# Residual tokens, P7's weights and the g_post products of the first output pair put into other places of a two-layer trunk's last stages

## The chip, the cores and the metric

The kernel runs on one core of a Trainium2 chip. The metric is the device time of one execution in microseconds (us), the lower the better; several executions are timed and the median is given. One further execution was recorded by the hardware profiler.

The engines that matter here are TensorE (PE: matmuls, and PEld: its weight loads), VectorE (DVE), ScalarE (ACT), GpSimd (POOL) and SyncE (SP, whose queue SPq issues most transfers between DRAM and the on-chip memory). Each engine executes its own instructions in the order in which they stand in its queue; an instruction that waits for a semaphore holds up all behind it on that engine.

## The reference

A trunk of two layers over 512 tokens of width 2048, all in float32. Each layer normalises its input, applies one combined input projection, runs a gated linear attention group and a chunked attention group, gates and concatenates their outputs, and applies one output projection, a second normalisation and the residual. The part that the change touches is the end:

```python
def hybrid_layer(x, w_in, w_out, g_pre, g_post, w_alpha, b_alpha, g_gla, g_att, rel_bias):
    B, S, _ = x.shape
    h = rmsnorm(x, g_pre)
    z = h @ w_in
    ...
    y = jnp.concatenate([o_gla, o_att], axis=-1) @ w_out
    return x + rmsnorm(y, g_post)

def rmsnorm(x, g):
    xf = x.astype(jnp.float32)
    y = xf * lax.rsqrt(jnp.mean(xf * xf, axis=-1, keepdims=True) + EPS) * g.astype(jnp.float32)
    return y.astype(x.dtype)
```

So the row sums of squares are taken over y before `g_post`, and the product with `g_post` may come before or after the scaling by the root.

## The kernel before

**Matmuls and jobs.** Every weight block is 2048 rows by 512 columns, cut into 8 chunks of 128 x 1024 (two rows of 128 x 512 side by side), 512 KB each. A float32 product is made of three: the weight chunk is split into `wh` (rounded, on ScalarE, line 195) and `wl` (the rest, on VectorE, line 203), the operand likewise, and TensorE adds hi by hi, hi by lo and lo by hi (line 384). A pair of blocks is computed with seven products P1 to P7 in place of eight; each product is four *jobs*, one for each chunk c = 0 to 3, and each job is 12 matmuls of 128 x 512. "P5 2" below is the job of P5 with chunk 2. P1 uses a weight chunk H alone; P5 and P6 add a second chunk `raw` into it (line 189); P3 uses P6's `raw`; P7 subtracts a chunk of its own from H (line 191); P2 and P4 use chunks of the first block. P5, P6, P3 and P7 also read sums of operands (`sa`, 512 KB, from the DRAM arrays oS), one tile for each job (line 176).

`Job.load` issues the transfers of a job on SyncE's queue, `Job.high` makes the addition or subtraction and `wh`, `Job.low` makes `wl`; they run a few jobs ahead of the matmuls. The buffers are rings: 4 for H, 5 for raw, 4 for sa, 4 for wh, 3 for wl, 8 for the small tiles t2 (128 x 512). A job's `wl` can be written when the matmuls of the job three before have read theirs.

**Output projection.** It has four blocks of 512 columns, in two pairs: W01 (columns 0 to 1023) and W23 (1024 to 2047). In both layers W01 goes through the seven products (`fast_gemm`); in the last layer W23 does too, in layer 0 it goes through `std_gemm`, one job after the other. The jobs of W23 in the last layer stand in this order:

```python
PROD_END = order("10 20 11 21 12 22 13 23 50 51 60 52 61 53 62 63 30 31 32 33 70 71 72 73 40 41 42 43")
```

The results come out as P2, P4, P3 and P7 finish, two token tiles each: `out_consume` calls `project`, which combines two results on VectorE (`combine`, line 341), takes the sum of squares on ScalarE (line 1301) and multiplies by `g_post` on VectorE (line 1304) into the slots `ys`: a122, a123, g8, g11 for W01 and g0 to g3 for W23. `finish_token` then forms the root, scales, adds the residual and writes the output. W01's gains are loaded into two tiles called bias in the linear-attention part of the layer; W23's are loaded into two t2 tiles at its start (line 1291).

**Residual tokens.** For token tiles 2 and 3 the layer's input is loaded into g9 and g10 (512 KB each) and into bias, bias, sg, sg (256 KB each): `load_tokens` lists the moves and `Tokens.load` issues some of them (line 452). In the last layer that is done behind P3 3 and P7's jobs (`residual`).

**P7's weights in W23.** They go to four spare slots, g12, g13, g16 and g17, and are fetched when P3's jobs are loaded.

**Order.** The order of the instructions on each engine is fixed when the program is built: a scheduler simulates a timeline and lines the instructions up in it; `tc.issue_after(x)` adds the condition that an instruction stands behind x. `pump` and `Pace` let side work (`tasks`, which yield) advance by steps between matmuls. `last_load`, `last_low`, `last_cast` and `last_mm` hold the latest instruction of that kind.

Of the kernel before, what the change touches and what calls it, by code (L numbers as in the profile page):

```python
# [7 lines left out]
F32 = mybir.dt.float32  # L8
# [7 lines left out]
P = 128  # L16
# [17 lines left out]
def hybrid_trunk(  # L34
# [30 lines left out]
    def nm(s):  # L65
        serial[0] += 1
        return f"{s}_{serial[0]}"
# [68 lines left out]
    last_cast, last_low, last_mm, last_load = [None], [None], [None], [None]  # L136

    class Job:
        def __init__(self, l, kind, c, b0, b1=None, pair=None):
# [13 lines left out]
        def load(self):  # L153
            k, c, p, b0, b1 = self.kind, self.c, self.pair, self.b0, self.b1
            end = b0 >= NB_IN and k != "std"
            if end:
                c = OC[c]
            top, bottom = (c + 4, c) if end else (c, c + 4)
            if k == "std":
                self.raw = self.fetch(rtile("raw", bufs=5), b0, c)  # L160
            elif k == "P1":
                p["H", self.c] = self.fetch(rtile("H"), b0, top)
            elif k == "P5":
                p["r", self.c] = self.fetch(rtile("raw", bufs=5), b1, top)
            elif k == "P6":
                p["r", self.c] = self.fetch(rtile("raw", bufs=5), b1, bottom)
            elif k == "P7":
                p["r", self.c] = p.pop(("t", self.c)) if b0 == W23[0] else self.fetch(rtile("raw", bufs=5), b0, top)
            elif k == "P2" or (k == "P4" and end):
                p["r", self.c] = self.fetch(rtile("raw", bufs=5), b0, bottom)  # L170
            sums = so_d if end else sa_d[self.l]
            src = sums.get((LEFT.get(k), c))
            if src is not None and b0 != NB_IN and not (k == "P5" and b0 == AV0):
                until(lambda: k == "P4" or (id(sums), LEFT[k], c) in written)
                self.a = rtile("sa", (2, 512), F32R)
                last_load[0] = nc.sync.dma_start(flat(self.a), src).ins
            if k == "P3" and b0 == W23[0]:
                with tc.issue_after(last_load[0]):
                    p["t", self.c] = self.fetch(slot(SPARE[self.c], [2, 512]), b0, c + 4)

        def high(self):
# [264 lines left out]
    XS1 = ("g9", "g10")  # L446

    class Tokens(list):
        def load(self, n=None):
            for z, src in self.moves[:n]:  # L450
                with tc.issue_after(last_load[0]):
                    nc.sync.dma_start(z, src)
            del self.moves[:n]

# [249 lines left out]
    def layer(l):  # L704
# [476 lines left out]
        def turn_gla(h, p):  # L1181
            ps = aux()
            for f in range(2):
                for tt in range(2):
                    nc.tensor.transpose(
                        ps[:, f * 256 + tt * P : f * 256 + (tt + 1) * P],
                        normed[h, p][:, tt, f * P : (f + 1) * P], ident,
                    )
            assert p or h >= 2 or ("P2", h) in passed
            op = slot(OG[p, h], [2, 512], F32R)  # L1190
            full_o = out_parts(h)[2 * p + 1]
            for f in range(2):
# [12 lines left out]

        def gla_heads(j, gvh, gvl):
            units = []
# [83 lines left out]
            nc.sync.dma_start(gp, bass.AP(tensor=src.tensor, offset=src.offset, ap=[[0, P], [1, W]]))  # L1291
            return gp

        def project(o, n, src, gp, between=None):
            if o not in ssy:
                ssy[o] = sm(5, "ssy", 4)
                nc.gpsimd.memset(ssy[o][:, 4:5], EPS)
            if (o, n // 2) not in ys:
                ys[o, n // 2] = slot(YS[n // 2][o], [1024])
            j = t2(dtype=BF16)  # L1300
            nc.scalar.activation(j, src, AF.Square, scale=D ** -0.5, accum_out=ssy[o][:, n : n + 1])
            if between is not None:
                between()
            nc.vector.tensor_tensor(
                out=ys[o, n // 2][:, (n % 2) * W : (n % 2 + 1) * W], in0=src, in1=gp, op=ALU.mult
            )

        def out_evac(n):
            gp = load_gain(n, t2())
# [42 lines left out]
        def out_consume(n):  # L1352
            if n:
                gains[:] = [load_gain(n + j, t2()) for j in range(2)]
            ends = []

            def f(j, h, t, src, comb):
                until(lambda: len(gains) == 2)
                o = 2 * h + t
                ending = last and n == 2 and (j, h) == (0, 1)  # L1360

                def begin():
                    ends.append(finish_token(o, xs[1][t]))
                    next(ends[-1])

                with nullcontext() if n and (j, h) == (0, 1) else tc.issue_after(last_low[0]):
                    project(o, n + j, src if comb is None else comb(t2()), gains[j], begin if ending else None)
                if last and n == 2 and (j, h, t) == (1, 0, 1):
                    tasks.append(finish(0, None))
                if ending:  # L1370
                    if t == 0:
                        next(ends[0])
                    else:
                        for end in ends:
                            for _ in end:
                                pass
            return f

        fast_gemm(l, W01, out_consume(0), rate=2, after=lambda k, c: used.add((k, c)), end=True, ops=O)
        drain()  # L1380

        def residual(k, c):
            if (k, c) == ("P3", 3):
                xs[1] = load_tokens(1, x_src)
            elif k == "P7":
                xs[1].load(2 if c > 1 else 1)

        if last:
            fast_gemm(
# [3 lines left out]
        else:  # L1393
            for half in range(2):
                for b in W23:
                    if b == W23[1]:
                        xs[half] = load_tokens(half, x_src)
                        xs[half].load()
# [65 lines left out]
```

## Time and profile before

| | us |
|---|---|
| three runs | 1640.9, 1643.17, 1645.68 (median 1643.17) |
| profiled execution | 1639.9 |
| its span from first to last instruction | 1637.8 |
| TensorE busy | 1613.9 |
| VectorE busy | 1253.2 |
| ScalarE busy | 911.4 |
| GpSimd busy | 122.0 |

The mean granted clock of TensorE in the profiled execution is 0.997 of full speed. Rows of the timeline read: start (us from the span's start), busy us, engine, line and operation, output <- inputs with partitions x elements, count; in square brackets the idle time of the engine just before, and what released it. Rows of windows read: the stretch, its length, the busy time of PE, PEld, DVE, ACT and POOL with the number of instructions, then TensorE's granted clock, the share of the DMA engines that was busy, and what they moved in GB/s.

### The profile page before, as it was taken

The numbers are of one execution on the slowest core, as the hardware profiler recorded it, in microseconds if no ns is written. First come the engines' busy times: TensorE is split into PE (matmuls) and PEld (weight loads), VectorE is DVE, ScalarE is ACT, GpSimd is POOL, SyncE is SP. The second block draws the span as 40 slices with busy tenths as digits, with TensorE's granted clock in tenths as the row PEclk, the third lists the DMA queues.
The fourth block names the chain that finished last, engine by engine and source line by source line (L and its number), as shares of the span: only waits on it lengthen the run. The fifth ranks groups of instructions, "written<-read, shape, count | busy, mean of one in ns | idle before, by whom it ended". The sixth has DMA issues, their size and how long they took to land.

```text
span 1637.8 us, 24501 instructions
## 1 busy us (share of the span) xinstructions
PE 1613.9 (99%) x8986; PEld 1382.4 (84%) x8986; DVE 1253.2 (77%) x1630; ACT 911.4 (56%) x1497; POOL 122.0 (7%) x182
## 2 busy tenths in 40 slices
PE   9999999999999999999999999999999999999996
PEld 7888999998888778788788889999988887787885
DVE  5987778687787868995786667776776878699976
ACT  7554445666554556654674444455665545566553
POOL 0120000100000100000122000000000101101001
PEclk9999999999999999999999999999999999999999
DMA  9698685785869667277989486858858596785967
GB/s 368 239 377 283 229 308 196 251 305 173 297 201 354 223 220 262 95 262 267 332 278 398 172 309 220 305 184 271 272 175 296 186 333 232 232 297 200 347 232 228
DMA packets 130759, 426.10 MB, mean 260 GB/s; under 512 B 14052, under 2 KB 26852, under 8 KB 130608
## 3 DMA queue, kind: packets, MB, share of 16 engines
q1 hardware_dynamic: 115632, 370.22, 65.2%
q0 software_dynamic: 14432, 53.24, 8.8%
q8 instruction: 71, 1.16, 0.3%
q10 hardware_dynamic: 576, 1.08, 0.2%
q14 instruction: 48, 0.39, 0.1%
HBM read 371.25 MB, written 55.33 MB: 260 GB/s over the span
## 4 chain that ended last, share of the span: by engine, by line
PE 89%; DVE 5%; DMA 4%; issue 1%; ACT 1%; DVEq 0%; POOL 0%; SPq 0%; ACTq 0%; POOLq 0%
PE mm L384 46%; PE mm L374 19%; PE mm L306 12%; PE ax L907 2%; DVE wl L203 1%; PE ax L384 1%; PE ax L1092 1%; DMA H<-in_w_dram 1%; PE ax L890 1%; DMA raw<-in_w_dram 1%; DMA x_mid<-g 1%; PE ax L1064 1%; DVE g L106 1%; PE ax L871 1%; PE ax L870 1%
## 5 line engine op out<-in xcount | busy, mean ns | idle before, releaser
L384 PE MATMUL mm<-wh,sa 128*128 128x512 f32 x1472 | 479.1, 395 | 6.4 <-DMA sa<-oS 4.8
L195 ACT CAST wh<-raw 128x1024 fp32r<-128x1024 f32 (+1 forms) x249 | 261.3, 1053 | 223.1 <-PE mm L384 88.1
L203 DVE TENSOR_TENSOR wl<-raw,wh 128x1024 fp32r<-128x1024 f32 (+1 forms) x249 | 302.5, 1218 | 92.2 <-PE mm L384 31.6
L195 ACT CAST wh<-H 128x1024 fp32r<-128x1024 f32 x240 | 251.6, 1051 | 212.2 <-PE mm L384 96.8
L203 DVE TENSOR_TENSOR wl<-H,wh 128x1024 fp32r<-128x1024 f32 x240 | 292.9, 1222 | 91.8 <-PE mm L384 34.4
L384 PEld LDWEIGHTS mm<-wh,sa 128*128 128x128 f32 x1472 | 276.5, 188 | 74.1 <-issue 11.7
L384 PE MATMUL mm<-wl,sa 128*128 128x512 f32 x736 | 288.9, 392 | 4.3 <-DVE wl L203 4.3
L374 PE MATMUL mm<-sa,wh 128*128 128x256 f32 x1280 | 236.8, 285 | 0.0
L384 PE MATMUL mm<-wh,a 128*128 128x512 f32 x608 | 200.5, 394 | 0.5 <-ACT wh L195 0.5
L374 PEld LDWEIGHTS mm<-sa,wh 128*128 128x128 f32 x1280 | 200.0, 191 | 0.3
L374 PE MATMUL mm<-sa,wl 128*128 128x256 f32 x640 | 181.1, 283 | 0.0
L189 DVE TENSOR_TENSOR H<-H,raw 128x1024 f32<-128x1024 f32 x132 | 160.3, 1221 | 7.9 <-DMA raw<-in_w_dram 6.6
L384 PEld LDWEIGHTS mm<-wl,sa 128*128 128x128 f32 x736 | 138.7, 188 | 32.5 <-DVE wl L203 5.4
L384 PEld LDWEIGHTS mm<-wh,a 128*128 128x128 f32 x608 | 113.5, 188 | 24.4 <-ACT wh L195 0.9
L374 PEld LDWEIGHTS mm<-sa,wl 128*128 128x128 f32 x640 | 122.5, 191 | 0.0
L425 POOL TENSOR_TENSOR sm<-sm,mhalf 128x2 f32<-128x2 f32 (+2 forms) x42 | 52.8, 1258 | 934.3 <-DVE sm L917 452.5
L384 PE MATMUL mm<-wl,a 128*128 128x512 f32 x304 | 119.8, 394 | 0.0
L191 DVE TENSOR_TENSOR raw<-H,raw 128x1024 f32<-128x1024 f32 x56 | 68.6, 1225 | 45.2 <-DMA raw<-in_w_dram 45.0
L374 PE MATMUL mm<-a,wh 128*128 128x256 f32 x512 | 95.3, 285 | 0.0
L306 PE MATMUL mm<-wh,a 128*128 128x512 f32 x288 | 91.5, 390 | 0.0
L384 PE MATMUL mm<-wh,g 128*128 128x512 f32 x288 | 90.9, 390 | 0.2 <-ACT wh L195 0.2
L208 DVE TENSOR_TENSOR H<-H,raw 128x1024 f32<-128x1024 f32 x48 | 58.7, 1224 | 33.2 <-DMA raw<-in_w_dram 33.2
(235 smaller groups left out, 2429.3 us busy)
## 6 DMA issues: line engine op xcount, KB each, us to landing
raw<-in_w_dram SPq DMA_DIRECT2D x319, 512.0 KB, 4.9
sa<-S SPq DMA_DIRECT2D x184, 512.0 KB, 4.4
H<-in_w_dram SPq DMA_DIRECT2D x60, 512.0 KB, 5.1
sa<-A SPq DMA_DIRECT2D x48, 512.0 KB, 6.1
S<-g POOLq DMA_DIRECT2D x32, 512.0 KB, 8.9
sa<-oS SPq DMA_DIRECT2D x16, 512.0 KB, 5.9
oa<-g POOLq DMA_DIRECT2D x12, 512.0 KB, 6.4
g<-in_x_dram SPq DMA_DIRECT2D x10, 512.0 KB, 9.1
```

The source lines that it names most:

```text
L106: return nc.vector.tensor_tensor(out=lo, in0=src, in1=hi.bitcast(F32), op=ALU.subtract).ins
L189: nc.vector.tensor_tensor(out=h, in0=h, in1=r, op=ALU.add)
L191: nc.vector.tensor_tensor(out=r, in0=h, in1=r, op=ALU.subtract)
L195: last_cast[0] = nc.scalar.copy(self.wh[:, z, :], src[:, z, :]).ins
L203: last_low[0] = nc.vector.tensor_tensor(out=self.wl[:, z, :], in0=self.src[:, z, :], in1=self.wh[:, z, :].bitcast(F32), op=ALU.subtract).ins
L208: nc.vector.tensor_tensor(out=h, in0=h, in1=self.src, op=ALU.add)
L306: nc.tensor.matmul(pss[o], a(part, kk, o) if callable(a) else a[:, part, t], rhs[:, kk, :], start=(i == 0 and kk == 0 and m == 0), stop=(i ...
L374: nc.tensor.matmul(dst, lhs[:, kk, f], a[:, part, tok], start=(fresh and kk == 0 and m == 0 and ft % 2 == 0), stop=(c == 3 and kk == 1 and ...
L384: last_mm[0] = nc.tensor.matmul(out_ps[t], a[:, part, tok], rhs[:, kk, :], start=(fresh and kk == 0 and m == 0), stop=(c == 3 and kk == 1 ...
L425: nc.gpsimd.tensor_tensor(out=out_r, in0=v, in1=mhalf[:, : v.shape[-1]], op=ALU.pow)
L870: nc.tensor.matmul(ps[:, :n], self.qh[:, t], self.kl[:, :n], start=False, stop=False)
L907: nc.tensor.matmul(o, self.pt[i][:, j * P : (j + 1) * P], av[hd // 4, j // 2][:, j % 2, (hd % 4) * P : (hd % 4 + 1) * P], start=(j == 0), ...
```

## The change

It has four parts.

1. In the last layer's W23, P7's own weights are fetched when P5's jobs are loaded, each behind `last_h`, the last H load of a P1 job, in place of when P3's jobs are loaded.
2. In the last layer the residual tokens are listed after P2 0, and one move is issued at each step of P1 and P2, behind `last_h`; before, they were listed after P3 3 and issued at P7's jobs. `Tokens.load` takes the instruction to stand behind as an argument.
3. W01 keeps y without `g_post`: the combination writes straight into the `ys` slot, P4's result is copied there by ScalarE, and the sum of squares reads y. W01's gains are no longer loaded in the linear-attention part, which leaves the bias tiles free for the tokens.
4. A task `late_gains`, put up in both layers when W01 is through, loads two gains into t2 tiles and multiplies the eight halves of W01's `ys` slots in place, one product after each three steps of the task, each behind `last_low`.

```diff
@@ -160,6 +160,7 @@
             elif k == "P1":
                 p["H", self.c] = self.fetch(rtile("H"), b0, top)
+                last_h[0] = last_load[0]
...
-            if k == "P3" and b0 == W23[0]:
-                with tc.issue_after(last_load[0]):
+            if k == "P5" and b0 == W23[0]:
+                with tc.issue_after(last_h[0]):
                     p["t", self.c] = self.fetch(slot(SPARE[self.c], [2, 512]), b0, c + 4)
@@ -446,9 +447,9 @@
     class Tokens(list):
-        def load(self, n=None):
+        def load(self, behind, n=None):
             for z, src in self.moves[:n]:
-                with tc.issue_after(last_load[0]):
+                with tc.issue_after(behind):
                     nc.sync.dma_start(z, src)
@@ -1198,10 +1199,6 @@
-            if len(og) == 8:
-                for n in range(2):
-                    gains.append(tmp.tile([P, W], F32, tag="bias", name=nm("bias"), bufs=2))
-                    load_gain(n, gains[n])
@@ -1291,19 +1288,32 @@
-        def project(o, n, src, gp, between=None):
+        def project(o, n, src, gp=None, comb=None, between=None):
...
+            dst = ys[o, n // 2][:, (n % 2) * W : (n % 2 + 1) * W]
+            y = src if comb is None else comb(dst if gp is None else t2())
+            if gp is None and comb is None:
+                nc.scalar.copy(dst, src)
             j = t2(dtype=BF16)
-            nc.scalar.activation(j, src, AF.Square, scale=D ** -0.5, accum_out=ssy[o][:, n : n + 1])
+            nc.scalar.activation(j, y, AF.Square, scale=D ** -0.5, accum_out=ssy[o][:, n : n + 1])
             if between is not None:
                 between()
-            nc.vector.tensor_tensor(
-                out=ys[o, n // 2][:, (n % 2) * W : (n % 2 + 1) * W], in0=src, in1=gp, op=ALU.mult
-            )
+            if gp is not None:
+                nc.vector.tensor_tensor(out=dst, in0=y, in1=gp, op=ALU.mult)
+
+        def late_gains():
+            gs = [load_gain(n, t2()) for n in range(2)]
+            for o in range(NT):
+                for n in range(2):
+                    for _ in range(3):
+                        yield
+                    dst = ys[o, 0][:, n * W : (n + 1) * W]
+                    with tc.issue_after(last_low[0]):
+                        nc.vector.tensor_tensor(out=dst, in0=dst, in1=gs[n], op=ALU.mult)
...
-                    project(o, n + j, src if comb is None else comb(t2()), gains[j], begin if ending else None)
+                    project(o, n + j, src, gains[j] if n else None, comb, begin if ending else None)
@@ -1378,12 +1387,13 @@
         fast_gemm(l, W01, out_consume(0), rate=2, after=lambda k, c: used.add((k, c)), end=True, ops=O)
         drain()
+        tasks.append(late_gains())
 
         def residual(k, c):
-            if (k, c) == ("P3", 3):
+            if (k, c) == ("P2", 0):
                 xs[1] = load_tokens(1, x_src)
-            elif k == "P7":
-                xs[1].load(2 if c > 1 else 1)
+            if k in ("P1", "P2") and xs:
+                xs[1].load(last_h[0], 1)
```

What this does to the order of SyncE's queue around the start of the last layer's W23, and of VectorE's some jobs later, is shown in three pieces. Names carry a tile's tag and a running number. First SyncE before the change, from the last H of W23's P1 jobs on:

```order
L150 DMA H_2956_15159<-in_w_dram 128x1024
L1291 DMA t2_2943_15115<-in_g_post_dram 128x512
L1291 DMA t2_2944_15117<-in_g_post_dram 128x512
L150 DMA raw_2966_15216<-in_w_dram 128x1024
L150 DMA raw_2970_15237<-in_w_dram 128x1024
L150 DMA raw_2974_15258<-in_w_dram 128x1024
L150 DMA raw_2980_15283<-in_w_dram 128x1024
L150 DMA raw_2990_15316<-in_w_dram 128x1024
```

The same place with the change:

```order
L150 DMA H_2944_15143<-in_w_dram 128x1024
L453 DMA g9_2945_15145<-x_mid_79 128x1024
L453 DMA g10_2946_15146<-x_mid_79 128x1024
L150 DMA g12_2958_15193<-in_w_dram 128x1024
L453 DMA bias_2947_15147<-x_mid_79 128x512
L150 DMA g13_2963_15218<-in_w_dram 128x1024
L453 DMA bias_2948_15148<-x_mid_79 128x512
L453 DMA sg_2949_15149<-x_mid_79 128x512
L150 DMA g16_2972_15266<-in_w_dram 128x1024
L1288 DMA t2_2929_15095<-in_g_post_dram 128x512
L1288 DMA t2_2930_15097<-in_g_post_dram 128x512
L1288 DMA t2_2938_15121<-in_g_post_dram 128x512
```

A fourth gain follows, and then the raws of P5 and P6; three of P7's four weights and five of the six token moves now stand between the last H and these raws. Before, both stood between the `sa` loads at the end of W23:

```order
L176 DMA sa_3010_15419<-oS40_134 128x1024
L150 DMA g16_3011_15421<-in_w_dram 128x1024
L150 DMA raw_3052_15604<-in_w_dram 128x1024
L452 DMA g10_3040_15556<-x_mid_79 128x1024
L150 DMA raw_3055_15626<-in_w_dram 128x1024
L176 DMA sa_3016_15443<-oS41_135 128x1024
L150 DMA g17_3017_15445<-in_w_dram 128x1024
L452 DMA bias_3041_15557<-x_mid_79 128x512
L452 DMA bias_3042_15558<-x_mid_79 128x512
L452 DMA sg_3043_15559<-x_mid_79 128x512
L176 DMA sa_3020_15463<-oS32_132 128x1024
```

These token moves and weights are gone from there with the change; only raws remain among the `sa` loads. On VectorE the eight late products (line 1316) stand, with the change, between the `wl` splits (line 204) of P2 3 and P6 1. From P2 3's split on, where `wl_2964` is P5 0's, `wl_2968` P5 1's and `wl_2975` P6 0's:

```order
L204 TENSOR_TENSOR wl_2959_15209<-raw_2953_15169,wh_2955_15187 128x1024
L1316 TENSOR_TENSOR a122_2859_14739<-a122_2859_14739,t2_2938_15121 128x512
L1316 TENSOR_TENSOR a123_2862_14745<-a123_2862_14745,t2_2938_15121 128x512
L1316 TENSOR_TENSOR a122_2859_14739<-a122_2859_14739,t2_2939_15123 128x512
L1316 TENSOR_TENSOR a123_2862_14745<-a123_2862_14745,t2_2939_15123 128x512
L204 TENSOR_TENSOR wl_2964_15234<-H_2906_14999,wh_2960_15212 128x1024
L1316 TENSOR_TENSOR g8_2910_15007<-g8_2910_15007,t2_2938_15121 128x512
L190 TENSOR_TENSOR H_2920_15051<-H_2920_15051,raw_2961_15214 128x1024
L190 TENSOR_TENSOR H_2906_14999<-H_2906_14999,raw_2966_15239 128x1024
L204 TENSOR_TENSOR wl_2968_15257<-H_2920_15051,wh_2965_15237 128x1024
L1316 TENSOR_TENSOR g8_2910_15007<-g8_2910_15007,t2_2939_15123 128x512
L192 TENSOR_TENSOR g12_2958_15193<-H_2906_14999,g12_2958_15193 128x1024
```

In this piece six late products and the first of P7's four subtractions (line 192, into g12) stand among the splits of P5; before, the products stood in W01 and this subtraction behind the `wl` of P3 0. The other subtractions stand, with the change, between the splits of P5 2 and P6 3; before, the last of them stood among those of P7.

More of the change, by code (lines that the diff above doesn't have):

```diff
@@ L135, in hybrid_trunk @@
     SPARE = ("g12", "g13", "g16", "g17")
-    last_cast, last_low, last_mm, last_load = [None], [None], [None], [None]
+    last_cast, last_low, last_mm, last_load, last_h = [None], [None], [None], [None], [None]
     class Job:
@@ L1357, in f @@
             def f(j, h, t, src, comb):
-                until(lambda: len(gains) == 2)
                 o = 2 * h + t
@@ L1397, in layer @@
                         xs[half] = load_tokens(half, x_src)
-                        xs[half].load()
+                        xs[half].load(last_load[0])
                     std_gemm(l, b, (2 * half, 2 * half + 1), OL, operand_out, out_evac(b - NB_IN), rate=3, lag=2)
```

## The prediction

> **What bounds the kernel now.** I read the page's head and engine totals first, then the waits of TensorE, then the timeline around the longest of them.
>
> ```profile
> span 1637.8 us, 24501 instructions
> PE 1613.9 (99%) x8986; PEld 1382.4 (84%) x8986; DVE 1253.2 (77%) x1630; ACT 911.4 (56%) x1497; POOL 122.0 (7%) x182
> ```
>
> TensorE is busy for 99% of the span, so only its holes can be won or lost (the profiled run took 1639.9 us, 2.1 outside the span). The waits of TensorE, as total, times and longest:
>
> ```profile
> PE mm L384 <- DMA sa<-oS: 4.8, 2, 3.2
> PE mm L384 <- DVE wl L203: 4.3, 2, 2.7
> ```
>
> The first is the only one on a transfer, and both its cases lie in the last layer's second output pair, W23:
>
> ```profile
> 1598.07 0.39 PE L384 MATMUL mm<-wh,sa 128*128 128x512 f32 x1
> 1601.66 0.47 PE L384 MATMUL mm<-wh,sa 128*128 128x512 f32 x1 [3.20 <-DMA sa<-oS]
> 1604.27 0.39 PE L384 MATMUL mm<-wh,sa 128*128 128x512 f32 x1
> 1606.25 0.47 PE L384 MATMUL mm<-wh,sa 128*128 128x512 f32 x1 [1.59 <-DMA sa<-oS]
> ```
>
> ```profile
> 1546.62 0.61 PE L384 MATMUL mm<-wh,a 128*128 128x512 f32 x2
> ...
> 1568.83 0.39 PE L384 MATMUL mm<-wl,sa 128*128 128x512 f32 x1
> ```
>
> The last two rows give TensorE's beat. From W23's first matmul to P5 0's first with wl lie 98 matmuls in 22.21 us: 0.227 each, 2.72 for a job of 12. Start to start the two gaps are 3.59 and 1.98; less one matmul each, they lose 3.36 + 1.75 = 5.1 us. Nothing behind them could take that up, as TensorE sets the end.
>
> Three stretches of W23 (length, then busy us of PE, PEld, DVE, ACT, POOL, clock, DMA share, GB/s) and SyncE's queue in the last tell why the sums were late:
>
> ```profile
> 1528.00:1550.00 22.00, 22.00 (x98) 18.20 (x97) 19.25 (x22) 13.06 (x23) 0.00 (x0) 1.00 1.01 396
> 1550.00:1582.00 32.00, 32.00 (x143) 26.48 (x142) 25.97 (x25) 14.97 (x18) 0.00 (x0) 1.00 0.59 190
> 1582.00:1608.00 26.00, 21.21 (x93) 16.98 (x92) 19.98 (x18) 11.28 (x14) 0.00 (x0) 1.00 0.97 362
> ...
> 1592.02 0.33 SPq L150 DMA_DIRECT2D g<-in_w_dram  x1
> 1593.82 1.64 SPq L452 DMA_DIRECT2D bias<-x_mid  x2
> ...
> 1597.75 0.32 SPq L176 DMA_DIRECT2D sa<-oS  x1
> ```
>
> ```profile
> DMA to landing us min/median/max: 3.6/7.8/10.5
> ```
>
> The DMA engines are full (0.97) from 1582 on and 0.59 busy before. The late sum is issued at 1597.75, and the sums of this stretch land a median 7.8 us after issue against 3.6 at best. Counted in SyncE's queue, 10.0 MB are issued there (8 sums, 4 of P7's weights and 3 raws of 0.52 MB, tokens of 2.1 MB), and 362 GB/s carry 9.4 in 26 us: the stretch is too short for them.
>
> **The change, part by part.**
>
> (a) P7's weights and the tokens move to the stretch around 1550. That takes 4 x 0.52 + 2.1 = 4.2 MB out of the full stretch; what stays, 5.8 MB, needs 16 of its 26 us. After the move each sum is behind raws alone in SyncE's queue. The latest of those raws wait until VectorE has read P6's raw tiles in P3, by my count at about 1595, and the sum behind needs to be there at 1602; even 4 us of landing fits. I take the whole 5.1 us as won. Its lower bound is one of the two waits, 3.36.
>
> (b) The transfers arrive where they are put. Ahead of the raws of W23's P5 and P6 now stand an H, most of the tokens, three of the four weights and four gains. Before, SyncE issued there:
>
> ```profile
> 1537.01 3.69 SPq L150 DMA_DIRECT2D H<-in_w_dram  x3
> 1540.81 1.61 SPq L1291 DMA_DIRECT2D t<-in_g_post_dram  x2
> ```
>
> ```profile
> DMA to landing us min/median/max: 9.0/9.0/9.0
> ```
>
> From the last H to the last gain that is 6 x 0.52 + 7 x 0.26 = 5.0 MB (H, two tokens, three weights; three small tokens, four gains). At the 396 GB/s of the full stretch, from about 1542 on with some backlog, it ends near 1557, and at worst near 1560 (the last third at 190). The last row is the landing of before's two gains, 9.0 us, so the backlog is real. VectorE wants the gains at 1561.4 (below): it just fits, at no cost. P5 1's raw behind them is wanted by VectorE only some ops later: nothing.
>
> (c) Eight products leave W01 and run in W23, and P7's four subtractions can run as soon as their weights are there. VectorE's rows give the price by distance of starts:
>
> ```profile
> 1540.25 0.69 DVE L1304 TENSOR_TENSOR g<-t,bias 128x512 f32<-128x512 f32 x1
> 1540.86 0.69 DVE L341 TENSOR_TENSOR t<-ev,ev 128x512 f32<-128x512 f32 x1
> ...
> 1562.04 1.22 DVE L203 TENSOR_TENSOR wl<-raw,wh 128x1024 fp32r<-128x1024 f32 x1
> 1563.17 1.22 DVE L203 TENSOR_TENSOR wl<-H,wh 128x1024 fp32r<-128x1024 f32 x1
> ...
> 1582.02 1.22 DVE L203 TENSOR_TENSOR wl<-H,wh 128x1024 fp32r<-128x1024 f32 x1 [1.49 <-PE mm L384]
> 1584.74 1.23 DVE L203 TENSOR_TENSOR wl<-raw,wh 128x1024 fp32r<-128x1024 f32 x1 [1.50 <-PE mm L384]
> ```
>
> ```profile
> 1546.60:1587.00 40.40, 40.40 (x180) 33.44 (x179) 31.37 (x30) 20.95 (x28) 0.00 (x0) 1.00 0.65 217
> ```
>
> 0.61 us for 512 columns, 1.135 for 1024. In W23's first 40.4 us VectorE is busy for 31.37: 9.0 are free. Two of the eight products were there before (P4's, by the order), so six more (3.6) and four subtractions (4.5) come to 8.2. By the sum they fit; by order they don't, because the free time is of the 1.49 kind: VectorE waits for a wl buffer that TensorE still reads. It can't run ahead of TensorE by more than three jobs, so what is lost in front is not made up.
>
> I therefore replayed VectorE's order against the beat. The wl of P2 3 is the eighth, and starts when job 5 gives its buffer back, 5 x 2.72 after 1546.62: 1560.2. It ends at 1561.4. Thirty operations follow back to back, up to the wl of P6 2: 12 of 512 columns and 18 of 1024, 12 x 0.605 + 18 x 1.135 = 27.7 us, so 1589.1. On the undisturbed beat TensorE needs that wl at 1546.62 + 14 x 2.72 + 0.45 = 1585.15. It stalls by 4.1 us up to there with the signal; in parts, at the wl of P5 2 (1577.7 against 1577.45, one job's two first matmuls being put ahead), of P6 1 (1581.8 against 1580.4, the first stall counted) and of P6 2. From P6 3 on the queue is ahead again. Bounds: two more matmuls put ahead at P6 2 would hide 0.45, so 3.7; by the busy time of 1.22 and 0.69 in place of the distances it is 30 x 0.085 more, 6.7. I take 4.1, the distances being what back-to-back operations show.
>
> (d) W01 becomes lighter by 6 to 8 products, but its stalls don't go: the 2.72 us wait for wl (its rows are under the clock) lies at 1504, before its first product. Two ScalarE copies of P4's result run beside matmuls (ScalarE is 56% busy): 0; without cover 2 x 0.6 a layer.
>
> (e) Layer 0's W23 is the standard product: one wl per job there too, VectorE idle for about half of each, and eight products at one per three yields: 0; at worst one 0.6 us operation late before a wl.
>
> Sum: -5.1 + 4.1 = -1.0, so 1638.9 for the profiled run, and 1642.2 by the median, as no other term differs between the two.
>
> **Clock.** A wait can cost more than itself:
>
> ```profile
> 1503.80 0.73 PE L384 MATMUL mm<-wh,sa 128*128 128x512 f32 x2 [0.30 <-ACT wh L195]
> 1507.26 0.50 PE L384 MATMUL mm<-wl,sa 128*128 128x512 f32 x1 [2.72 <-DVE wl L203]
> ...
> 1511.70 0.62 PE L384 MATMUL mm<-wh,g 128*128 128x512 f32 x2
> ```
>
> ```profile
> 1509.00:1511.00 2.00, 2.00 (x6) 1.52 (x6) 2.00 (x4) 1.45 (x5) 0.00 (x0) 0.50 0.00 0
> 1601.60:1603.60 2.00, 1.94 (x9) 1.62 (x10) 0.77 (x1) 0.00 (x0) 0.00 (x0) 1.00 1.05 393
> 1606.20:1608.20 2.00, 1.95 (x9) 1.66 (x10) 2.00 (x4) 0.73 (x2) 0.00 (x0) 1.00 1.03 409
> ```
>
> After the wait at 1504 the granted clock was 0.50, and from 1507.26 to 1511.70 TensorE did 12 matmuls, 2.7 us' worth on the beat: another 1.7 us lost. After the 3.6 us gap at 1598 the clock stayed at 1.00, and after the 2.0 us gap at 1604 too. My largest new gap is near 2.3 us, nearer to the last: I put 0 into the sum, 1.7 into the range. The Trainium skill, "TensorE: Matmul & The Clock Gate" (Part 1), says that the clock halves after an idle window of about 3.4 us, and that this window runs freely. That one of two gaps of about this length dropped it fits a window that isn't tied to the gap; by that rule a 2.3 us gap adds nothing, and the sum and the forecast stay.
>
> **The rivals.**
>
> A, faster: the jam on VectorE doesn't stop TensorE. For it: 9.0 us free against 8.2 added. Against it: the free time is not usable ahead. Price: -5.1, giving 1638.1, or up to 1 us less of that.
>
> B, slower: the gains come late, and VectorE's in-order queue stops behind its first late product. For it: the 9.0 us landing with far less ahead of it. Against it: 396 GB/s carry the 5.0 MB by 1557. Each us after 1561.4 is a us of stall, as the jam has no slack; from 0.9 us on the change is slower than before. With landings 4 us late, and a clock drop for what is then a gap of over 3 us: -1.0 + 4 + 1.7 = +4.7, 1647.9.
>
> C: the change doesn't do what it says, and the sums still wait (behind the raws that VectorE's jam delays), while the jam is paid: with one wait left -3.36 + 4.1 = +0.7, with none gone +4.1, 1647.3.
>
> **How the numbers follow.** The forecast's case has 0.54, A 0.21, B 0.17, C 0.08. About 0.3%, 4.9 us, is what a measurement of this kernel can tell from no change. Most of A lies beyond that, and a little of the forecast where the jam is smaller: faster 0.20. Half or more of B and C lie beyond on the other side, with the forecast's corner of a 6.7 us jam and a clock drop (-5.1 + 6.7 + 1.7 = +3.3, short of it by less than the spread of three runs): slower 0.21. The rest, 0.59, can't be told apart. Range: 1637 (A, with 1 us for the spread of the runs) to 1648.5 (B). The likeliest case alone goes from 1641.8 (-5.1 + 3.7) to 1646.5 (+3.3).
>
> **What would show it.** Right: no wait on sa<-oS left in TensorE's waits, DMA share below 0.8 from 1582 on; new waits on wl or wh of 3 to 5 us in all between 1577 and 1590, with VectorE busy without a break from 1560 to 1589 and back to waits on TensorE after it. A: no such waits. B: VectorE idle on a gain before its first late product. C: sa<-oS again in the list. I am wrong if a new wait shows up in W01 or in layer 0, or a total beyond the range.

## The result, and the profile after

| | median us | lowest to highest | runs |
|---|---|---|---|
| before | 1642.3 | 1640.45 to 1645.68 | 9 |
| with the change | 1636.26 | 1634.14 to 1639.86 | 9 |

The ratio is 0.9963, with a 95% interval from 0.9952 to 0.9974: 6.0 us faster, where 1.0 was forecast, and below the range (1637.0 to 1648.5). The profiled execution took 1638.54 us (span 1636.5), which is only 1.4 less than that of before. Two questions follow: which part of the change brought the gain, and why the medians differ by more than the two traces.

**The second output pair did what the prediction says.** The waits of TensorE with the change (total, times, longest; L385, L196 and L204 are the former L384, L195 and L203):

```profile
PE mm L385 <- DVE wl L204: 3.6, 4, 1.8
PE mm L385 <- ACT wh L196: 3.1, 2, 2.1
```

The sums are gone from the list. In W23's timeline stand three new gaps instead:

```profile
1575.89 0.50 PE L385 MATMUL mm<-wl,sa 128*128 128x512 f32 x1 [0.22 <-DVE wl L204]
...
1579.97 0.50 PE L385 MATMUL mm<-wl,sa 128*128 128x512 f32 x1 [1.04 <-DVE wl L204]
...
1587.40 0.98 PE L385 MATMUL mm<-wh,sa 128*128 128x512 f32 x2 [2.11 <-ACT wh L196]
```

The third is put down to ScalarE, but the `wl` of P6 2, which the prediction names for this place, ended on VectorE at 1587.33, 0.07 ahead of the matmul, and the `wl` of P5 2 and P6 1 ended as shortly ahead of the first two. So VectorE is read as the cause of all three: it worked back to back from the first late product on, and was first ahead of TensorE again in P3:

```profile
1558.32 1.23 DVE L204 TENSOR_TENSOR wl<-raw,wh 128x1024 fp32r<-128x1024 f32 x1 [1.50 <-PE mm L385]
1559.46 2.49 DVE L1316 TENSOR_TENSOR a<-a,t 128x512 f32<-128x512 f32 x4
...
1586.11 1.22 DVE L204 TENSOR_TENSOR wl<-H,wh 128x1024 fp32r<-128x1024 f32 x1
...
1594.61 1.23 DVE L204 TENSOR_TENSOR wl<-raw,wh 128x1024 fp32r<-128x1024 f32 x1 [1.50 <-PE mm L385]
```

The transfers went where they were sent, and TensorE's clock fell behind the last gap (columns as before: length, PE, PEld, DVE, ACT, POOL, clock, DMA share, GB/s):

```profile
1550.00:1582.00 32.00, 30.75 (x135) 24.77 (x134) 27.32 (x29) 12.12 (x15) 0.00 (x0) 1.00 0.84 311
1582.00:1608.00 26.00, 23.89 (x99) 19.26 (x98) 21.02 (x21) 13.20 (x17) 0.00 (x0) 0.93 0.64 222
...
1589.50:1591.00 1.50, 1.50 (x5) 1.21 (x4) 1.50 (x3) 0.00 (x0) 0.00 (x0) 0.50 0.00 0
```

So in these two traces W23 gave 5.1 us and took 4.1 for the gaps and 1.7 for the half clock: nothing is left.

**The first output pair became shorter, in both layers.** Ahead of the gap near 688 and after it, before:

```profile
688.44 0.73 PE L384 MATMUL mm<-wh,sa 128*128 128x512 f32 x2 [1.36 <-ACT wh L195]
690.78 0.50 PE L384 MATMUL mm<-wl,sa 128*128 128x512 f32 x1 [1.61 <-DVE wl L203]
```

With the change, there and in the last layer (2.72 before):

```profile
687.13 0.73 PE L385 MATMUL mm<-wh,sa 128*128 128x512 f32 x2 [0.94 <-ACT wh L196]
688.39 0.50 PE L385 MATMUL mm<-wl,sa 128*128 128x512 f32 x1 [0.53 <-DVE wl L204]
...
1504.66 0.50 PE L385 MATMUL mm<-wl,sa 128*128 128x512 f32 x1 [1.82 <-DVE wl L204]
```

That is 1.5 us in layer 0 and 0.9 in the last. Nothing in these rows names a transfer. But on VectorE there is no idle time between 1479 and 1507; the last idle time ahead of the gap is this one, before and with the change, in the last layer and in layer 0:

```profile
1479.24 2.36 DVE L189 TENSOR_TENSOR H<-H,raw 128x1024 f32<-128x1024 f32 x2 [2.44 <-DMA raw<-in_w_dram]
...
661.51 1.23 DVE L189 TENSOR_TENSOR H<-H,raw 128x1024 f32<-128x1024 f32 x1 [2.52 <-DMA raw<-in_w_dram]
```

```profile
1475.39 1.22 DVE L190 TENSOR_TENSOR H<-H,raw 128x1024 f32<-128x1024 f32 x1 [1.06 <-DMA raw<-in_w_dram]
...
658.68 1.23 DVE L190 TENSOR_TENSOR H<-H,raw 128x1024 f32<-128x1024 f32 x1 [0.54 <-DMA raw<-in_w_dram]
```

VectorE waited for a weight chunk. What stands ahead of that chunk in SyncE's queue, first before, then with the change:

```profile
1463.60 1.50 SPq L150 DMA_DIRECT2D raw<-in_w_dram  x2
1470.41 0.33 SPq L1291 DMA_DIRECT2D bias<-in_g_post_dram  x1
1470.84 0.85 SPq L150 DMA_DIRECT2D raw<-in_w_dram  x2
1476.18 0.33 SPq L1291 DMA_DIRECT2D bias<-in_g_post_dram  x1
```

```profile
1462.63 14.34 SPq L150 DMA_DIRECT2D raw<-in_w_dram  x5
```

Before, W01's two gain loads stood among the raws of W01. Each waited until TensorE's transposes in the linear attention (line 1185) had read the bias tile that it goes to; this is SyncE's wait for that over both layers:

```profile
SPq L1291 <- PE ax L1185: 18.9, 4, 5.0
```

That wait itself delays little: from the two raws ahead of the first gain to the two behind it pass 7.2 and 6.6 us, and 6.7 and 6.6 with the change, where no gain stands between them. So one raw is issued 0.6 us later. The larger part is the landing of these two raws. First the last layer and layer 0 before, then layer 0 with the change:

```profile
DMA to landing us min/median/max: 7.8/7.8/7.8
DMA to landing us min/median/max: 5.6/6.0/6.4
...
DMA to landing us min/median/max: 4.4/4.4/4.4
```

In the three us behind the first of them the DMA engines moved less than half as much as with the change (before, then with the change):

```profile
1470.90:1473.90 3.00, 3.00 (x15) 2.48 (x14) 2.60 (x3) 3.00 (x7) 0.00 (x0) 1.00 0.37 115
1469.40:1472.40 3.00, 3.00 (x17) 2.52 (x15) 2.60 (x3) 3.00 (x8) 0.00 (x0) 1.00 0.79 244
```

A gain load reads the same 2 KB of DRAM for all 128 partitions (line 1291 of the kernel before). Whether this is what slows the raws behind it, no run tests. The change takes these loads away from there.

### The profile page after: what moved, and what is told of

It reads as the page before. It is cut to its first block, busy times and chain, and to the rows that moved or that the text cites. A ratio compares the mean times of both kernels' runs of the same rounds, so it can differ in the third digit from the quotient of the medians.

```text
span 1636.5 us, 24496 instructions
## 1 busy us (share of the span) xinstructions
PE 1615.8 (99%) x8986; PEld 1383.6 (85%) x8986; DVE 1251.5 (76%) x1630; ACT 911.8 (56%) x1501; POOL 120.9 (7%) x182
## 4 chain that ended last, share of the span: by engine, by line
PE 92%; DVE 3%; DMA 3%; issue 1%; ACT 1%; SPq 0%; POOL 0%; DVEq 0%; ACTq 0%; POOLq 0%
PE mm L385 47%; PE mm L375 19%; PE mm L307 14%; PE ax L908 2%; PE ax L385 1%; DVE wl L204 1%; PE ax L1093 1%; PE ax L891 1%; PE ax L728 1%; PE ax L1065 1%; DMA x_mid<-g 1%; PE ax L872 1%; PE ax L871 1%; PE ax L870 1%; DMA H<-in_w_dram 1%
## 5 line engine op out<-in xcount | busy, mean ns | idle before, releaser
L385 PE MATMUL mm<-wh,sa 128*128 128x512 f32 x1472 | 479.9, 396 | 3.1 <-ACT wh L196 3.1
L196 ACT CAST wh<-raw 128x1024 fp32r<-128x1024 f32 (+1 forms) x249 | 261.2, 1053 | 229.4 <-PE mm L385 94.2
L204 DVE TENSOR_TENSOR wl<-raw,wh 128x1024 fp32r<-128x1024 f32 (+1 forms) x249 | 301.8, 1215 | 93.4 <-PE mm L385 35.0
L196 ACT CAST wh<-H 128x1024 fp32r<-128x1024 f32 x240 | 251.5, 1050 | 213.8 <-PE mm L385 98.0
L204 DVE TENSOR_TENSOR wl<-H,wh 128x1024 fp32r<-128x1024 f32 x240 | 292.0, 1219 | 95.7 <-PE mm L385 38.2
L385 PEld LDWEIGHTS mm<-wh,sa 128*128 128x128 f32 x1472 | 277.2, 189 | 70.3 <-issue 8.5
L385 PE MATMUL mm<-wl,sa 128*128 128x512 f32 x736 | 289.5, 393 | 3.6 <-DVE wl L204 3.6
L385 PE MATMUL mm<-wh,a 128*128 128x512 f32 x608 | 200.7, 394 | 0.0
L385 PEld LDWEIGHTS mm<-wl,sa 128*128 128x128 f32 x736 | 138.9, 189 | 32.5 <-DVE wl L204 5.3
L190 DVE TENSOR_TENSOR H<-H,raw 128x1024 f32<-128x1024 f32 x132 | 159.7, 1217 | 6.2 <-DMA raw<-in_w_dram 5.0
L385 PEld LDWEIGHTS mm<-wh,a 128*128 128x128 f32 x608 | 113.5, 188 | 23.7 <-ACT wh L196 0.3
L385 PE MATMUL mm<-wl,a 128*128 128x512 f32 x304 | 119.8, 394 | 0.0
L385 PE MATMUL mm<-wh,g 128*128 128x512 f32 x288 | 90.9, 389 | 0.0
L337 ACT COPY ev<-mm 128x512 f32<-128x512 f32 x96 | 56.1, 584 | 57.1 <-PE mm L385 40.8
```

The lines of the kernel that those rows point to most:

```text
L190: nc.vector.tensor_tensor(out=h, in0=h, in1=r, op=ALU.add)
L196: last_cast[0] = nc.scalar.copy(self.wh[:, z, :], src[:, z, :]).ins
L204: last_low[0] = nc.vector.tensor_tensor(out=self.wl[:, z, :], in0=self.src[:, z, :], in1=self.wh[:, z, :].bitcast(F32), op=ALU.subtract).ins
L337: nc.scalar.copy(e, src[t])
L385: last_mm[0] = nc.tensor.matmul(out_ps[t], a[:, part, tok], rhs[:, kk, :], start=(fresh and kk == 0 and m == 0), stop=(c == 3 and kk == 1 ...
```

## The experiments

Each kernel was timed beside the kernel before on one chip. The median of that kernel stands with each group.

**e1: the kernel before again.** No edit.

> The unchanged kernel again. Question: is the one profiled execution of it (1639.9 us, below all nine timed runs, 1640.45 to 1645.68) a lucky one? Theory 1 (clock): the difference of the medians, -6.0 us against the -1.3 us that the two traces show, is made by windows of 3.41 us at half clock, 1.7 us each, which follow TensorE's gaps of 3.1 and 3.6 us in some executions and not in others; then the mean clocks of the runs lie between 0.995 and 0.998, a trace shows the half clock behind 1598 as well in about half the cases, and the time falls with the clock. Theory 2 (W01): the clock has nothing to do with it, the runs' clocks are alike, and the difference lies in the first output pairs, where VectorE does less. Either way the ratio is 1.000 within 0.001.

Measured: 1641.78 us against 1640.61 of 34 runs; ratio 1.001 [1.000, 1.0019]. The mean clock of the runs goes from 0.992 to 0.997 and falls as the time rises (correlation -0.6). The windows of this trace at 688, 1505 and 1604 show half clock behind three gaps, where the first trace of this kernel had it behind one only, at 1504:

```profile
690.00:696.00 6.00, 5.53 (x13) 4.38 (x14) 6.00 (x9) 3.76 (x6) 0.00 (x0) 0.50 0.18 42
1509.00:1512.00 3.00, 3.00 (x9) 2.33 (x8) 3.00 (x5) 2.45 (x6) 0.00 (x0) 0.51 0.20 82
1604.50:1607.50 3.00, 3.00 (x9) 2.32 (x8) 1.23 (x1) 0.00 (x0) 0.00 (x0) 0.50 1.04 401
```

What follows: the profiled execution of before was one with few half-clock stretches, and that of the changed kernel was the second slowest of its nine runs, so the difference of two traces is not that of the medians.

**e2: only the transfers of W23 are moved** (the diff's first part, and two of the six token moves; the others stay at P7):

```diff
...
-            if (k, c) == ("P3", 3):
+            if (k, c) == ("P2", 0):
                 xs[1] = load_tokens(1, x_src)
+            if k in ("P1", "P2") and xs and len(xs[1].moves) > 4:
+                xs[1].load(last_h[0], 1)
             elif k == "P7":
-                xs[1].load(2 if c > 1 else 1)
+                xs[1].load(last_load[0], 1)
```

> Only the transfers are moved (P7's weights, and two of the six token moves; the other four stay at P7's jobs, since W01's gains keep the bias tiles); the g_post products stay in W01. Theory 1: both waits for the sums go (-5.1 us), and with eight late products fewer (4.8 us) the jam on VectorE is down to 0 to 0.5 us: ratio 0.996 to 0.997 and by the clock up to 0.995. Theory 2: the W01 part of the gain is missing, and W01's gaps near 686 and 1504 stay as before (3.8 and 3.1 us from start to start): 0.998 to 0.999.

**e3: only the products with g_post are moved** (the diff's third and fourth part).

```diff
-            if k == "P5" and b0 == W23[0]:
-                with tc.issue_after(last_h[0]):
+            if k == "P3" and b0 == W23[0]:
+                with tc.issue_after(last_load[0]):
...
-            if (k, c) == ("P2", 0):
+            if (k, c) == ("P3", 3):
                 xs[1] = load_tokens(1, x_src)
-            if k in ("P1", "P2") and xs:
-                xs[1].load(last_h[0], 1)
+            elif k == "P7":
+                xs[1].load(last_load[0], 2 if c > 1 else 1)
```

> Only the g_post products are moved (W01 keeps y, late products in W23); P7's weights and the tokens stay where they were. Theory 1: the waits for the sums stay (4.8 us idle), no jam since the subtractions of P7 stay late: ratio 0.999 to 1.001. Theory 2: W01's gaps shrink in both layers, 3.8 to 2.3 us near 686 and 3.1 to 2.2 us near 1504 as in the changed kernel's trace, ratio 0.998 to 0.9985.

Measured for e2: 1638.27 us, ratio 0.9988 [0.9978, 0.9997]; for e3: 1637.75 us, 0.9987 [0.9975, 0.9998]. The waits for the sums in e2, then in e3:

```profile
PE mm L385 <- DMA sa<-oS: 0.7, 1, 0.7
```

```profile
PE mm L385 <- DMA sa<-oS: 5.1, 2, 2.9
```

In e2 W01's gaps are those of before (1.72 and 2.00 us from start to start at 686, 3.10 at 1504); in e3 they are 1.33, 0.92 and 1.55. e2's ratio is that of theory 2; e3's lies between the two ranges. In the traces the gain in W01 comes with the products' part of the change, as theory 2 has it, and the sums' waits go with the transfers. e2's trace is 4.2 us shorter than that of before, but its median only 2.3: the traced execution is the fastest of its ten, and what the others lose is not known. In e2, with the subtractions of P7 early but no late products, VectorE is busy without a break from 1563 to 1592 and yet in time: the only gap left in W23 is the 0.7 us for a sum.

**e4: the changed kernel with P7's subtractions late**, in all pairs:

```diff
                 elif k == "P7":
-                    nc.vector.tensor_tensor(out=r, in0=h, in1=r, op=ALU.subtract)
+                    with tc.issue_after(last_low[0]):
+                        nc.vector.tensor_tensor(out=r, in0=h, in1=r, op=ALU.subtract)
```

> The changed kernel with P7's subtractions put behind the latest wl split on VectorE, so that they no longer stand among the splits of P5 and P6. Both theories of the jam: with four 1.135 us operations out of the way the two new gaps (1.2 and 2.3 us lost near 1578 and 1585) go, and nothing else changes: -3.5 us against the changed kernel, and the half-clock window behind 1587 (1.7 us) goes too where it came: ratio to before 0.993 to 0.9945. Rival: the jam is made by the eight late products, not by the subtractions: then half of the two gaps stays, ratio 0.9955.

Measured: 1641.98 us, ratio 1.0008 [0.9999, 1.0018]. The gain that was expected did not come: W23 has no gap over 0.7 us any more, but the other pairs' subtractions were held back too, and TensorE now waits for wl in W01 at 1525, 1530 and 1534, 5.1 us in all.

**e5: the kernel before, with W01's gains behind the raws of P6.** This takes from the change nothing but the place of two loads in each layer:

```diff
-            if len(og) == 8:
-                for n in range(2):
-                    gains.append(tmp.tile([P, W], F32, tag="bias", name=nm("bias"), bufs=2))
-                    load_gain(n, gains[n])
...
-        fast_gemm(l, W01, out_consume(0), rate=2, after=lambda k, c: used.add((k, c)), end=True, ops=O)
+        def first_gains(k, c):
+            used.add((k, c))
+            if (k, c) == ("P6", 1):
+                for n in range(2):
+                    gains.append(tmp.tile([P, W], F32, tag="bias", name=nm("bias"), bufs=2))
+                    with tc.issue_after(last_load[0]):
+                        load_gain(n, gains[n])
+
+        fast_gemm(l, W01, out_consume(0), rate=2, after=first_gains, end=True, ops=O)
```

> The kernel before with one thing changed: W01's two gains are loaded behind the raws of P6 in W01 (SyncE) and no longer ahead of two raws of P1 and P2, where SyncE waits until the bias tiles are free. Late products, W23's loads and the rest stay as before. Theory W (the early gains' place in SyncE's queue holds the raws up, VectorE loses 2.4 us to that at 1477 and 2.5 at 659, works back to back from there, and TensorE pays at 1504 and 688): VectorE's wait for a raw shrinks to 0.4 to 1.1 us in both layers, the gaps near 686 go from 3.8 to about 2.3 us and near 1504 from 3.1 to about 1.6 to 2.2 us, ratio 0.998 to 0.9985, by the clock windows behind 688 and 1504 down to 0.997. Theory P (it is the moved products that lighten W01): gaps and time as before, ratio 1.000.

**e6: the changed kernel, with the early gain loads put back.** Nobody reads them; the late products load their own.

```diff
+            if len(og) == 8:
+                for n in range(2):
+                    load_gain(n, tmp.tile([P, W], F32, tag="bias", name=nm("bias"), bufs=2))
```

> The changed kernel with the two early gain loads put back at their old place into bias tiles that nobody reads (0.5 MB more per layer, no product with them). Theory W: SyncE waits there again, VectorE's waits of 2.4 us come back, the gaps near 686 and 1504 are as in the kernel before (3.8 and 3.1 us), and it is 2.5 to 5 us slower than the changed kernel, ratio to before 0.998 to 0.9995. Theory P: as the changed kernel, 0.9963.

**e7: the changed kernel with the subtractions late in W23 alone.**

```diff
                 elif k == "P7":
-                    nc.vector.tensor_tensor(out=r, in0=h, in1=r, op=ALU.subtract)
+                    with tc.issue_after(last_low[0]) if self.b0 == W23[0] else nullcontext():
+                        nc.vector.tensor_tensor(out=r, in0=h, in1=r, op=ALU.subtract)
```

> The changed kernel with P7's four subtractions put behind the latest wl split in W23 alone (the pin on all pairs made new waits for wl in W01 at 1525 to 1536, 6 us, while W23 lost its two new gaps). No gap over 0.7 us from 1510 to 1610, W01 as in the changed kernel: 3.5 us less than the changed kernel, 5 with the clock window behind 1587; ratio to before 0.993 to 0.9945. Rival (TensorE pays the saved time elsewhere in W23, at the sums or the late products): ratio 0.996.

**e8: the changed kernel again.** No edit.

> The changed kernel again beside the others on one chip. Ratio 0.995 to 0.9975. Question: how many half-clock windows its runs have against those of the kernel before; by the clock theory its mean clock lies 0.001 to 0.002 above that of the kernel before, one or two windows of 1.7 us.

Measured, all four beside one set of 34 runs of the kernel before (1640.47 us, mean clock 0.9952):

| | median us | ratio | interval | mean clock of its runs |
|---|---|---|---|---|
| e5 gains behind the raws | 1635.82 | 0.9970 | 0.9959 to 0.9981 | 0.9972 |
| e6 changed, early gains back | 1642.28 | 1.0014 | 1.0001 to 1.0027 | 0.9948 |
| e7 changed, subtractions late | 1635.85 | 0.9968 | 0.9957 to 0.9979 | 0.9964 |
| e8 changed | 1637.48 | 0.9973 | 0.9963 to 0.9983 | 0.9976 |

The recorded ratio need not be the quotient of the two medians (0.9982 for e8). e5 brings 4.7 us with the place of two loads alone, where the whole change brings 3.0 on this chip; their intervals overlap, so the two are not told apart. e6, which has all of the change but that, loses the gain again, 4.8 us behind e8, and is not faster than the kernel before (its ratio is above the 0.998 to 0.9995 that was expected). SyncE's queue, VectorE's wait and TensorE's gap in the last layer of e5:

```profile
1461.85 19.95 SPq L150 DMA_DIRECT2D raw<-in_w_dram  x6
1481.89 0.86 SPq L1287 DMA_DIRECT2D bias<-in_g_post_dram  x2
...
1474.35 1.23 DVE L189 TENSOR_TENSOR H<-H,raw 128x1024 f32<-128x1024 f32 x1 [0.81 <-DMA raw<-in_w_dram]
...
1503.63 0.50 PE L384 MATMUL mm<-wl,sa 128*128 128x512 f32 x1 [1.58 <-DVE wl L203]
```

and in e6:

```profile
1472.69 0.33 SPq L1291 DMA_DIRECT2D bias<-in_g_post_dram  x1
1473.13 0.85 SPq L150 DMA_DIRECT2D raw<-in_w_dram  x2
...
1481.47 2.36 DVE L190 TENSOR_TENSOR H<-H,raw 128x1024 f32<-128x1024 f32 x2 [2.38 <-DMA raw<-in_w_dram]
...
1509.48 0.80 PE L385 MATMUL mm<-wl,sa 128*128 128x512 f32 x1 [2.71 <-DVE wl L204]
```

The gain comes and goes with the two loads, with the products in either place; theory P is out. Theory W has the right loads and the right places, but one link is other than it says: not the hold in the queue is large, but the landing. In the four traces with the early loads (before, e1, e2, e6) the two raws behind the first gain land 7.0 to 7.8 us after issue in the last layer. VectorE's addition, where it waits for the first of them, starts 7.8 to 8.4 us after that issue, and 5.4 to 6.1 in the traces without the loads. In layer 0 the landing takes 5.6 to 6.8 us in before, e1 and e2, and 4.1 to 4.8 in all nine traces without the loads.

The gaps are 2.6 us shorter in e5 (1.5 in layer 0, 1.1 in the last). The clock adds to that: behind the gaps near 688 and 1504 the four traces with the early loads have ten half-clock stretches, each of which loses 1.7 us, 4.3 us for a trace; the nine without them have one in all (with the change, at 1505). The mean clocks point the same way: 0.002 of 1640 us is 3.3 us, a part of it behind the last matmul, where it costs nothing. Together this is more than the 4.7 measured, so the traces give both parts but not their shares. In W23, where nothing was edited, e5's trace has one wait for a sum of 3.1 us, against 4.8 and 3.8 in the two traces of the kernel before; a part of the 4.7 may lie there. e6 also prices W23 as the change leaves it: with W01 as in the kernel before it is not faster.

e7 has no gap over 0.7 us in W23, and its last matmul starts at 1618.5 against 1625.8 in e8. Yet its span is only 2.7 us shorter, the ratio is near the rival's (0.996) and above the one expected, and its interval overlaps that of e8. Its end, the token sums, GpSimd's output transfers of tokens 0 and 1, and the window around the last matmul:

```profile
1608.20 0.15 DVE L1330 TENSOR_REDUCE sm<-ssy 128x1 f32<-128x5 f32 x1
...
1612.03 0.96 POOL L1343 DMA_DIRECT2D out_dram<-a  x1 [0.80 <-ACT a L1342]
...
1616.00:1624.00 8.00, 2.90 (x13) 2.07 (x11) 6.38 (x10) 1.43 (x5) 1.77 (x3) 0.99 1.04 193
```

The late subtractions had pushed the token sums (L1330) back on VectorE. So these transfers started as late as in the changed kernel (1611.3 in its first trace, 1610.6 in e8), 6 us before the last matmul in place of 15, and ran into the last stores, with the DMA engines full (1.04): 14.5 us from the last matmul to the end in place of 9.9.

**e9: e2 and e5 together**, the products where they were before.

> e2 and e5 together: W01's gains behind the raws, P7's weights and two of the token moves early in W23, all products with g_post where they were before. If the two effects are separate places of the program, they add: W01 as in e5 (gaps of 2.3 near 686 and 1.6 to 2.2 near 1504), W23 as in e2 (one gap near 1.1 us in place of 5.1 us of waits, no half-clock window there), ratio 0.9975 x 0.9975 = about 0.995 (0.9935 to 0.996), 1632 to 1634 us. Rival: the end of W23 is set by the output transfers, which issue at a time that the sums' waits don't move; then W23 gives nothing and the ratio is that of e5 alone, 0.997.

Measured: 1635.41 us against 1640.44; ratio 0.9965 [0.9954, 0.9976]. The two effects were expected to add (0.9935 to 0.996). They do not: W01 is that of e5, but W23 has a gap again, with half clock behind it. VectorE's row ahead of it, and the gap:

```profile
1583.04 1.22 DVE L190 TENSOR_TENSOR H<-H,raw 128x1024 f32<-128x1024 f32 x1 [2.30 <-DMA raw<-in_w_dram]
...
1586.59 0.50 PE L385 MATMUL mm<-wl,sa 128*128 128x512 f32 x1 [2.45 <-DVE wl L204]
```

The row is P4 1's addition, which the scheduler had put, with that of P4 0 at 1579.52, among the splits of P6; its weight chunk had not landed, and the splits behind it waited. That is the same pattern a third time, an early operation ahead of needed ones. The rival (the output transfers set the end) is not what happened: the end follows the last matmul by 10.0 us.

**e10 and e11: e9 with the subtractions late in W23**, in e10 as in e7, in e11 right behind the last wl of P6:

```diff
+            if self.kind == "P6":
+                last_p6[0] = last_low[0]
...
+                    with tc.issue_after(last_p6[0]) if self.b0 == W23[0] else nullcontext():
                         nc.vector.tensor_tensor(out=r, in0=h, in1=r, op=ALU.subtract)
```

> e9 with P7's four subtractions behind the latest wl split, in W23 alone. The jam theory: e9's gap of 2.85 us (start to start) near 1584 goes, and the half-clock window behind it, 4.3 us earlier at the last matmul. Then the end: in e7, where TensorE was done early, the span went on for 14.5 us after the last matmul in place of 9.9, since the outputs of tokens 0 and 1 were issued as late as before and met the last stores. If that holds here, 4.5 us are lost again and the ratio stays at 0.9965; if the end follows the last matmul by 10 us it is 0.994.

> As e10, but the subtractions stand right behind the last wl of P6, so that VectorE makes them in P3, where it waits 1.5 us of each 2.7 for TensorE, and is free for P3's results and the token sums earlier than in e10. The jam theory: four subtractions (4.5 us) in a row ahead of P3 0's wl; VectorE is at most three jobs ahead there, so 0 to 1.5 us of wait for that wl. The end: the token sums come one or two operations earlier than in e10, so 0 to 2 us better there. Ratio 0.9935 to 0.9965.

Measured beside 1642.16 us: e10 1634.98, ratio 0.9958 [0.9946, 0.997]; e11 1632.07, ratio 0.9937 [0.9925, 0.9949]. With the subtractions tied down, P4 0's addition stands behind P3 0's split, and both have lost the gap. e10's interval still overlaps that of e9, and its ratio lies between the two that were expected; e11's is at the fast end of its range. e10 ends 13.9 us behind its last matmul, as e7 does; in e11 the token sums run at 1601.9 and the same transfers start early, the DMA engines are not full around the last matmul, and it is 9.9 us again:

```profile
1601.88 0.15 DVE L1319 TENSOR_REDUCE sm<-ssy 128x1 f32<-128x5 f32 x1
...
1604.57 0.96 POOL L1332 DMA_DIRECT2D out_dram<-a  x1 [0.98 <-ACT a L1331]
...
1616.00:1624.00 8.00, 3.68 (x17) 2.69 (x15) 5.60 (x9) 1.38 (x4) 1.10 (x2) 1.00 0.66 182
```

e11, which keeps all products in W01, beats the kernel before by 10 us (five runs) and has its interval wholly below both that were measured of the change.

## Why the prediction was wrong

It forecast a change of -1.0 us, and the sign held; the time lay below its range because one term was put at 0.

- **(a) The sums' waits, -5.1.** Right in the traces: none is left with the change, and they stay in e3, which doesn't move the transfers. What that is worth in the medians is less sure: e2, with 0.7 us of these waits left and no jam, gained only 2.3.
- **(b) Landings.** Right. VectorE started the late products at 1559.46, with no wait for a gain; rival B did not come, and rival C neither.
- **(c) The jam, +4.1.** Right in size, place and parts. From start to start the three gaps are 0.61, 1.42 and 2.50 us; less a matmul each, and with 0.11 twice for a slower matmul behind a wait, 4.1. e2 and e7 show that it takes both halves: without the late products VectorE is in time, and so it is with them when the subtractions are late.
- **The clock, taken as 0.** Wrong on both sides: the half clock came behind the third gap in both traces of the changed kernel and in e6, 1.7 us, and also behind the waits for the sums in e1, e3 and e5, though not in the first trace. On balance W23 is worth nothing, as e6 shows.
- **(d) "W01 becomes lighter by 6 to 8 products, but its stalls don't go."** This is the step that failed. It argued from VectorE's order alone, that no product stands ahead of the wait at 1504, and put the term at 0. It did not cost what the change takes out of SyncE's queue: W01's two early gain loads, behind which the raws landed 7.8 us after issue in the last layer. The stalls at 688 and 1504 were the far end of that, carried through 27 us of VectorE work without a break. They became 1.5 and 0.9 us shorter; e5 prices the term, clock included, at 4.7 us.
- **The sum** then ran against one profiled execution. That of the kernel before had a single half-clock stretch ahead of its last matmul, where e1's has four in three places; so gaps that were shortened are worth more in the medians than in the two traces.

Not settled is how much of e5's gain is gaps and how much clock, as the mean clocks cover the whole span and all but two kernels have one trace each; and why raws land late behind a gain load.

## What to carry to other kernels

When a change removes a load, price the place it leaves in its queue: what stood behind it, how much later that was issued and how much later it landed. A stall that names a compute engine may start at a transfer much earlier: follow that engine back to its last idle time, and read what ended that. Work moved off the end of a stage should go where the engine is known to wait, with its order tied down; left to find its place as soon as its data are there, it stood here ahead of work that TensorE needed.

## What the runs showed of the hardware that was not expected

Half-clock stretches of about 3.4 us follow gaps well below that length: idle times of 1.82 us (at 1504 with the change) and 2.11 us (at 1587) brought them on, and the 3.20 us at 1598 in the first trace did not. The first of them, in the trace of the changed kernel:

```profile
1505.80:1509.20 3.40, 3.40 (x10) 2.62 (x9) 3.40 (x5) 2.71 (x7) 0.00 (x0) 0.50 0.10 40
```

"TensorE: Matmul & The Clock Gate" of the Trainium skill (Part 1) asks for an idle window of about 3.4 us, running freely, before the clock halves, and for a busy window of that length before it rises again. The stretches' length agrees (3.4 us here); that a whole idle window is needed does not, as the gaps measured here are shorter. Where a gap of 2 us costs 1.7 more in some runs, shortening it is worth, by this estimate, up to about twice what the wait shows.

Raws that stood in the queue right behind a load of one 2 KB row into 128 partitions landed 7.0 to 7.8 us after issue in the last layer's W01. The cause is open.
